# A two-pass MLP on one core: the second eighth's weights split piece by piece, the first pass's DMA queue written out by hand, and four buffers for the gated weights

## The chip, the core and the metric

The kernel runs on one core of a Trainium2 chip. The core has TensorE (matrix products into eight PSUM banks), VectorE, ScalarE and GpSimd (element-wise work; in the profile DVE, ACT and POOL) and SyncE, whose queue (SPq in the profile) issues nearly every DMA. The metric is the device time in microseconds, the median of several runs.

## The reference

One transformer-like layer with 1024 tokens and width 1024, all in float32. The change lies in its last third, the MLP (c and the six modulation rows come from a small projection at the start):

```python
h = (_rms(x) * (1.0 + scale_f) + shift_f)
u = jnp.square(jax.nn.relu(jnp.einsum('bsd,df->bsf', h, w_mlp_in[l])))   # 1024x1024 by 1024x4096
x = x + gate_f * jnp.einsum('bsf,fd->bsd', u, w_mlp_out[l])              # 1024x4096 by 4096x1024
```

## The kernel before, in words

**A float32 product** is made of three passes of TensorE: each operand is split into a rounded part and a rest (`split_w`, L137: a ScalarE cast, L138, then a VectorE subtraction, L139), and hi by hi, hi by lo and lo by hi are summed in PSUM.

**The first pass** computes `u` in eight eighths of 512 columns. An eighth is one step of Strassen's scheme in Winograd's form on 2x2 blocks: seven products (`one`, `two`, `six`, `five`, `seven`, `three`, `four`, L1124 to L1185) of 24 matmuls of 128x128 by 128x512 each instead of eight products, with sums of blocks before (`tees`, L1142; L1156, L1157) and after. The four blocks of an eighth's weights are called 11, 12, 21 and 22, `b["2"]` is a further sum. The activations' seven operands (A11, A12, S1 to S4, A22) are made once and kept, split, in 14 of 18 large buffers (tag `s8`, 8 KB in each partition). The weights' split pairs have two buffers (`mr`), the loaded blocks 21, 12 and 22 five (`f4`), block 11 two (`raw`). The results `ua` and `ub` (`s8`) go to DRAM (`put`, L1120).

**The start** of the first pass overlaps the end of the projection before it: its last two groups, `woB0` and `woB1`, are evicted from PSUM (L955), added to x by GpSimd (L956), and the rows of x are normalised (`h2_norm`, L974) and turned by TensorE (`h2_turn`, L992) three tokens' blocks at a time (`HI`, tokens' blocks 5, 6 and 7) between the first products of eighths 0 and 1. In that stretch, L1239 to L1251, the orders of TensorE, ScalarE and VectorE are written out by hand; instructions from outside of it may be put between.

**Beside the first pass** GpSimd multiplies the rows of `w_mlp_out` by the gate row (`gate_load`, `gate_times`, `gate_store`, L1190 to L1209), in 32 pieces of 128 rows: a 512 KB load, two or three multiplications or subtractions of 128x512, two 256 KB stores to `wd_d`. It has two buffers, and two pieces in every three products.

**The order of everything else** is chosen by a list scheduler on a simulated timeline: whatever the program's order offers first and the simulation holds ready is next on its engine. That holds for SyncE's queue too, but for the loads and stores of the gates, whose order among themselves is the program's. An engine then works its instructions in that order and waits at each for its operands. A load waits in the queue for its buffer to be free.

**The second pass** does the same on `u` and `wd_d`, four quarters of seven products of 48 matmuls (`product`, L1286; matmuls at L1304). Loads of its operands (`load`, L1271) and of x (`x2b`) begin as the buffers of the first pass come free; `t_two` (L1330) is a difference that GpSimd makes for the third product.

## Time and profile before

| | |
|---|---|
| median of 3 runs | 1380.03 us (1377.92 to 1384.39) |
| profiled execution | 1383.38 us, of which 1381.6 us are the span from first to last instruction |
| busy in the span | TensorE 93%, VectorE 71%, ScalarE 37%, GpSimd 33% |
| mean granted TensorE clock | 0.975 of 2.4 GHz |

The profile gives one execution. Times within it are microseconds from the span's start. A row of a timeline gives start, duration, engine, line, operation, written tile <- read tiles, shape, count, and in brackets how long the engine had been idle and what released it. A matmul's own duration (0.39) is longer than its distance to the next one, since matmuls are pipelined.

### The profile page before, as it was taken

How to read it: one execution, taken by the hardware profiler on the slowest of the kernel's cores; microseconds unless marked ns; L12 is line 12 of the kernel's file. 1: busy time of each engine (PE TensorE's matmuls, PEld its weight loads, DVE VectorE, ACT ScalarE, POOL GpSimd, SP SyncE). 2: the span in 40 equal slices, each digit the busy share in tenths (PEclk: the TensorE clock that was granted, in tenths of full speed). 3: DMA queues.
4: the chain of work that ended last, by engine and by line, in shares of the span. 5: the costliest groups of instructions: out<-in, count | busy, mean ns of one | idle time of the engine just before them, and what ended most of it. 6: DMA issues, size and time to landing. Idle time of an engine off the chain costs nothing. (4 is left out here: it accounts for less than half of the span.)

```text
span 1381.6 us, 16679 instructions
## 1 busy us (share of the span) xinstructions
PE 1288.2 (93%) x6131; PEld 1042.5 (75%) x6131; DVE 974.7 (71%) x1486; ACT 515.8 (37%) x801; POOL 460.4 (33%) x364
## 2 busy tenths in 40 slices
PE   5899899999999899999976898889999899999998
PEld 3678777888888666678864786678888778888887
DVE  6758897476754367753687574668867989888883
ACT  3642212343333366652544432222334242424240
POOL 1129451156622013322340034644553714050500
PEclk9899999999999999999997999999999999999999
DMA  9656566534357574832550348667669450514202
GB/s 292 187 126 164 151 171 141 132 100 139 115 168 174 140 166 116 291 138 78 181 168 16 107 160 263 218 221 234 234 208 354 179 215 29 199 46 152 92 31 92
DMA packets 123601, 220.51 MB, mean 160 GB/s; under 512 B 9896, under 2 KB 70376, under 8 KB 117888
## 3 DMA queue, kind: packets, MB, share of 16 engines
q1 hardware_dynamic: 100640, 202.68, 47.8%
q10 hardware_dynamic: 22880, 16.78, 3.9%
q8 instruction: 48, 0.79, 0.2%
q14 instruction: 33, 0.27, 0.1%
HBM read 159.55 MB, written 48.34 MB: 150 GB/s over the span
## 5 line engine op out<-in xcount | busy, mean ns | idle before, releaser
L1304 PE MATMUL V<-sb,sa 128*128 128x512 f32 x768 | 180.3, 392 | 6.0 <-DVE sb L139 4.7
L1201 POOL TENSOR_TENSOR wg<-wg,gf 128x512 f32<-128x512 f32 x64 | 107.5, 1703 | 223.1 <-DMA wg<-in_w_mlp_out_dram 120.0
L1304 PEld LDWEIGHTS V<-sb,sa 128*128 128x128 f32 x768 | 145.1, 189 | 37.8 <-DVE sb L139 5.9
L135 POOL TENSOR_TENSOR sm<-sm 128x8 f32<-128x8 f32 (+2 forms) x48 | 62.0, 1298 | 138.5 <-DVE sm L253 48.8
L1304 PE MATMUL U<-sb,sa 128*128 128x512 f32 x384 | 88.8, 389 | 0.0
L1304 PEld LDWEIGHTS U<-sb,sa 128*128 128x128 f32 x384 | 72.1, 188 | 14.9
L138 ACT CAST sb<-b 128x1024 fp32r<-128x1024 f32 x40 | 40.7, 1052 | 103.5 <-PE V L1304 57.5
L238 DVE SCALAR_TENSOR_TENSOR wa<-wa,sm 128x128 f32<-128x128 f32 (+1 forms) x154 | 72.4, 470 | 3.3
L1330 POOL TENSOR_TENSOR wdt<-b,t 128x1024 f32<-128x1024 f32 x8 | 24.3, 3060 | 136.9 <-DMA b<-wd_d 136.9
L1282 DVE TENSOR_TENSOR x2b<-V,x2b 128x512 f32<-128x512 f32 x64 | 42.5, 683 | 35.0 <-PE V L1304 35.0
L711 DVE CUSTOM_DVE_ANT_0 p<-S,wh 128x512 f32<-128x512 f32 (+3 forms) x96 | 49.9, 552 | 24.1 <-DMA wh<-nc_d 16.2
L139 DVE TENSOR_TENSOR sa<-a,sa 128x2048 fp32r<-128x2048 f32 x20 | 60.3, 3015 | 4.2 <-ACT sa L138 4.1
L139 DVE TENSOR_TENSOR sb<-b,sb 128x1024 fp32r<-128x1024 f32 x40 | 55.4, 1410 | 3.5 <-ACT sb L138 1.6
L701 POOL TENSOR_SCALAR_AFFINE_SELECT wh<-wh 128x128 f32<-128x128 f32 x64 | 18.2, 293 | 108.2 <-DVE sm L711 53.1
L723 ACT ACTIVATE p<-p,sm 128x1024 f32<-128x1024 f32 (+7 forms) x64 | 49.1, 770 | 4.4 <-DVE sm L719 3.7
L707 PE MATMUL S<-kt,qt 128*128 128x512 f32 (+3 forms) x96 | 38.7, 408 | 9.2 <-DVE sm L711 6.6
L138 ACT CAST sa<-a 128x2048 fp32r<-128x2048 f32 x20 | 38.2, 1911 | 22.3 <-DVE a L1327 11.0
L1304 PE MATMUL W<-sb,sa 128*128 128x512 f32 x192 | 45.1, 389 | 0.0
L743 PE MATMUL pt<-ident,p 128*128 128x128 f32 x288 | 40.6, 282 | 2.6 <-ACT p L723 2.6
L743 PEld LDWEIGHTS pt<-ident,p 128*128 128x128 f32 x288 | 31.7, 142 | 13.4 <-issue 8.1
L1304 PEld LDWEIGHTS W<-sb,sa 128*128 128x128 f32 x192 | 36.1, 188 | 7.5
L752 PE MATMUL av<-pT,fv 128*64 128x256 f32 (+1 forms) x320 | 40.2, 373 | 0.0
(391 smaller groups left out, 3449.3 us busy)
## 6 DMA issues: line engine op xcount, KB each, us to landing
wu<-in_w_mlp_in_dram SPq DMA_DIRECT2D x32, 512.0 KB, 4.5
wg<-in_w_mlp_out_dram SPq DMA_DIRECT2D x32, 512.0 KB, 4.8
wd_d<-wg SPq DMA_DIRECT2D x64, 256.0 KB, 3.6
a<-u_d SPq DMA_DIRECT2D x12, 1024.0 KB, 6.4
b<-wd_d SPq DMA_DIRECT2D x12, 1024.0 KB, 7.1
wa<-in_w_ada_dram ACTq DMA_DIRECT2D x10, 1024.0 KB, 5.7
wam<-in_w_ada_dram SPq DMA_DIRECT2D x16, 512.0 KB, 7.7
u_d<-ua SPq DMA_DIRECT2D x16, 512.0 KB, 3.0
```

Source lines behind the costliest of these rows:

```text
L135: G.tensor_tensor(ap, ap, mhalf.to_broadcast([P, n]), op=ALU.pow)
L138: A.copy(h_ap, raw_ap)
L139: eng.tensor_tensor(l_ap, raw_ap, f32(h_ap), op=ALU.subtract)
L238: V.scalar_tensor_tensor(w[:, 0], w[:, j], c_act[:, j : j + 1], w[:, 0], op0=ALU.mult, op1=ALU.add)
L707: T.matmul(sp[n], qt[:, n, dg], kt[:, n, c_], start=True, stop=False)
L711: V.tensor_tensor_reduce(ps[n][:, c_], sp[n], wh[:, n, c_], -1.0, 3.4e38, op0=ALU.add, op1=ALU.min, accum_out=mcs[n][c0 // CH])
L723: A.activation(ps[n][:, :W], ps[n][:, :W], AF.Exp, bias=mcs[n][0], scale=-1.0, accum_out=den[:, 2 * i + n : 2 * i + n + 1],)
L743: T.transpose(tp[:, n, i * P : (i + 1) * P], ps[i][n][:, j * P : (j + 1) * P], ident)
L752: T.matmul(av[own, at], fox_pair_of("fv", pr)[:, j, n * FD : (n + 1) * FD], pts[j][:, n, i0 * P :], start=(j == 0), stop=(j == 2 * gg + 1),)
L1201: G.tensor_tensor(w[:, hf], w[:, hf], gf[hf], op=ALU.mult)
L1282: V.tensor_tensor(xs, banks[i], xs, op=ALU.add)
L1304: T.matmul(banks[i], sa[pa][:, a, ii], sb[pb_][a // 2][:, a % 2, :], start=(first and a == 0 and m == 0), stop=(a == 3 and m == 2), skip_g ...
```

## The change

It edits five things. (1) `xn`, the normalised rows of tokens' blocks 0 to 4, takes buffers of tag `r2` (four) and no longer of `t2` (three), which the evictions of `woB` use too; the gate row `gf` goes the other way. (2) Eighth 1's block 22 and its sum `2` are kept as two half-size tiles each in `r2`, no longer in one `s8` buffer, so their load, splits and sums run in halves (`minus`). (3) In the stretch written by hand, eighth 1's splits of 11 and 21 stand right behind the work that frees their buffers, eighth 0's split of `2` at the end, and the sums that end `two` (`end_two`) behind the stretch. (4) From the fifth product on, the order of SyncE's queue is written out too: in each step the gate's store of two steps before, the gate's load, the weights' loads, and then the result stores of the step before. The gates take one piece in every step, from step 12 to step 45, in four buffers (two in one `s8` buffer, two in `r2`), and each load is two of 256 KB. (5) In the second pass `t1` and `b22` are loaded before `a12` and `b21`, `t_two` is made before the first product, and two of the four loads of x move behind the load of `a22`.

```diff
--- before.py
+++ after.py
@@ -978,7 +978,7 @@
         A.activation(ra([P, D], f"x2sq{t}"), xt, AF.Square, accum_out=rr)
         V.tensor_scalar(rr, rr, 1.0 / D, EPS, op0=ALU.mult, op1=ALU.add)
         rsqrt_(rr, 1)
-        xn = [t2([P, CH], f"xn{t}{n}") for n in range(2)] if t < 5 else None
+        xn = [r2([P, CH], f"xn{t}{n}") for n in range(2)] if t < 5 else None
         if xn is None:
             v = s8([P, D], f"xn{t}")
             V.tensor_scalar(v, xt, rr, None, op0=ALU.mult)
@@ -1070,6 +1070,19 @@
     NE = 8
     W2 = 2 * P
 
+
+    stores = []
+
+    def pieces(w):
+        return w if isinstance(w, list) else [w]
+
+    def minus(dst, u, v):
+
+        if any(isinstance(w, list) for w in (dst, u, v)):
+            dst, u, v = (w if isinstance(w, list) else [w[:, 0:2], w[:, 2:4]] for w in (dst, u, v))
+        for a, b, c_ in zip(pieces(dst), pieces(u), pieces(v)):
+            V.tensor_tensor(a, b, c_, op=ALU.subtract)
+
     class Eighth:
         def __init__(self, e):
             self.e = e
@@ -1081,17 +1094,25 @@
                 if name in names:
                     r, c_ = int(name[0]) - 1, int(name[1]) - 1
                     if self.e == 1 and name == "22":
-                        both = s8([P, 2, 4, W2], "wu1_22")
-                        self.b["2"], w = both[:, 0], both[:, 1]
+                        w = self.halves(name)
                     else:
                         w = make([P, 4, W2], f"wu{self.e}_{name}")
                     self.b[name] = w
                     at = self.e * CH + c_ * W2
-                    Q.dma_start(w, wup_v[:, 4 * r : 4 * r + 4, at : at + W2])
+                    n = 4 // len(pieces(w))
+                    for i, v in enumerate(pieces(w)):
+                        Q.dma_start(v, wup_v[:, 4 * r + n * i : 4 * r + n * i + n, at : at + W2])
+
+        def halves(self, name):
+
+            return [r2([P, 2, W2], f"wu{self.e}_{name}{i}") for i in range(2)]
 
         def halve(self, name):
             s = self.split[name] = mr([P, 2, 4, W2], f"wu{self.e}s{name}", F32R)
-            split_w(self.b[name], s[:, 0], s[:, 1])
+            w = pieces(self.b[name])
+            n = 4 // len(w)
+            for i, v in enumerate(w):
+                split_w(v, s[:, 0, n * i : n * i + n], s[:, 1, n * i : n * i + n])
 
         def product(self, left, name, banks, first):
             if name not in self.split:
@@ -1119,7 +1140,7 @@
 
         def put(self, n, st):
             at = self.e % 2 * 2 * CH
-            Q.dma_start(u_d[self.e // 2][n][:, at : at + 2 * CH], st.rearrange("p f c -> p (f c)"))
+            stores.append(lambda: Q.dma_start(u_d[self.e // 2][n][:, at : at + 2 * CH], st.rearrange("p f c -> p (f c)")))
 
         def one(self):
             self.X = [self.make[f](f"X{self.e}_{f}") for f in range(2)]
@@ -1132,19 +1153,22 @@
         def two(self):
             Y = [self.make[2 + f](f"Y{self.e}_{f}") for f in range(2)]
             self.product("A12", "21", Y, True)
+            self.Y = Y
             if self.e > 1:
                 self.tees()
+                self.end_two()
+
+        def end_two(self):
             for f in range(2):
-                V.tensor_tensor(self.c11[:, f], Y[f], self.c11[:, f], op=ALU.add)
+                V.tensor_tensor(self.c11[:, f], self.Y[f], self.c11[:, f], op=ALU.add)
                 self.square(self.c11, f)
             self.put(0, self.c11)
 
         def tees(self):
             b = self.b
             V.tensor_tensor(b["12"], b["12"], b["11"], op=ALU.subtract)
-            if self.e != 1:
-                b["2"] = ra([P, 4, W2], f"wt{self.e}")
-            V.tensor_tensor(b["2"], b["22"], b["12"], op=ALU.subtract)
+            b["2"] = self.halves("2") if self.e == 1 else ra([P, 4, W2], f"wt{self.e}")
+            minus(b["2"], b["22"], b["12"])
 
         def six(self):
             self.product("S2", "2", self.X, False)
@@ -1153,8 +1177,8 @@
             for f in range(2):
                 A.copy(self.c12[:, f], self.X[f])
             b = self.b
-            V.tensor_tensor(b["11"], b["2"], b["11"], op=ALU.subtract)
-            V.tensor_tensor(b["21"], b["21"], b["2"], op=ALU.subtract)
+            minus(b["11"], b["2"], b["11"])
+            minus(b["21"], b["21"], b["2"])
 
         def five(self):
             self.Z = [self.make[2 + f](f"Z{self.e}_{f}") for f in range(2)]
@@ -1190,23 +1214,26 @@
     def gate_load(n):
         if not gf:
             for hf in range(2):
-                gf.append(r2([P, CH], f"gf{hf}"))
+                gf.append(t2([P, CH], f"gf{hf}"))
                 Q.dma_start(gf[hf], rows_d[1, hf * CH : (hf + 1) * CH].partition_broadcast(P))
-            wg.append(s8([P, 2, 2, CH], "wg"))
-        tc.keep_in_program_order(Q.dma_start(wg[0][:, n % 2].rearrange("p h c -> p (h c)"), wdn_v[:, n, :]))
+            t = s8([P, 2, 2, CH], "wg")
+            wg.extend([t[:, i, hf] for hf in range(2)] for i in range(2))
+            wg.extend([r2([P, CH], f"wg{i}{hf}") for hf in range(2)] for i in range(2))
+        for hf in range(2):
+            Q.dma_start(wg[n % 4][hf], wdn_v[:, n, hf * CH : (hf + 1) * CH])
 
     def gate_times(n):
-        w = wg[0][:, n % 2]
+        w = wg[n % 4]
         for hf in range(2):
-            G.tensor_tensor(w[:, hf], w[:, hf], gf[hf], op=ALU.mult)
+            G.tensor_tensor(w[hf], w[hf], gf[hf], op=ALU.mult)
         if n % 4 < 2:
-            G.tensor_tensor(w[:, 1], w[:, 1], w[:, 0], op=ALU.subtract)
+            G.tensor_tensor(w[1], w[1], w[0], op=ALU.subtract)
 
     def gate_store(n):
         e, c_, f = n // 4, n // 2 % 2, n % 2
         at = (e % 2 * 2 + f) * CH
         for hf in range(2):
-            tc.keep_in_program_order(Q.dma_start(wd_d[e // 2][2 * c_ + hf][:, at : at + CH], wg[0][:, n % 2, hf]))
+            Q.dma_start(wd_d[e // 2][2 * c_ + hf][:, at : at + CH], wg[n % 4][hf])
 
     eighths = [Eighth(e) for e in range(NE)]
     e0, e1 = eighths[:2]
@@ -1218,7 +1245,7 @@
         steps += [lambda e=e, n=n: getattr(eighths[e], n)() for n in ("one", "two", "six", "five", "seven", "three", "four")]
     side = [[] for _ in range(len(steps) + 4)]
     for n in range(32):
-        at = 2 + n // 2 * 3 + n % 2
+        at = 12 + n
         for d, what in ((0, gate_load), (1, gate_times), (2, gate_store)):
             side[at + d].append(lambda what=what, n=n: what(n))
 
@@ -1237,32 +1264,39 @@
     for e in (e0, e1):
         e.load(("12", "22"))
     with tc.manual_schedule(engines={ENG.PE, ENG.Activation, ENG.DVE}):
-        for n, t in enumerate(HI):
-            if n == 0:
-                e0.one()
-            elif n == 1:
-                e0.two()
-            else:
-                e1.one()
-            h2_turn(t, xn[t])
-            make_s2(t)
-            if n == 0:
-                e0.tees()
+        e0.one()
+        h2_turn(HI[0], xn[HI[0]])
+        make_s2(HI[0])
+        e0.tees()
+        e1.halve("11")
+        e0.two()
+        h2_turn(HI[1], xn[HI[1]])
+        make_s2(HI[1])
+        e1.halve("21")
+        e1.one()
+        h2_turn(HI[2], xn[HI[2]])
+        make_s2(HI[2])
         e1.two()
+        e0.halve("2")
     e1.tees()
+    e0.end_two()
     split_part("S1", "r21", whole)
+    e1.end_two()
     split_part("A22", "r22", whole)
     r22, r12, r11 = (h2r[r] for r in ("r22", "r12", "r11"))
     V.tensor_tensor(r22, r22, r11, op=ALU.subtract)
     split_part("S3", "r22", whole)
     V.tensor_tensor(r12, r12, r11, op=ALU.subtract)
     split_part("S4", "r12", whole)
-    for n, step in enumerate(steps):
-        step()
-        for what in side[n]:
+    with tc.manual_schedule(engines={ENG.SP}):
+        for n, step in enumerate(steps):
+            due = list(stores)
+            stores.clear()
+            step()
+            for what in side[n] + due:
+                what()
+        for what in sum(side[len(steps) :], []) + stores:
             what()
-    for what in sum(side[len(steps) :], []):
-        what()
 
     x2b = []
     for q in range(4):
@@ -1313,21 +1347,24 @@
         def two(name):
             return lambda g: blk[name][:, 2 * g : 2 * g + 2]
 
-        for name in ("a11", "b11", "a12", "b21"):
+        for name in ("a11", "b11", "t1", "b22", "a12", "b21"):
             load(name)
+
+        def load_x2(n):
+            x2b.append(s8([P, 2, D], f"x2b{n}"))
+            Q.dma_start(x2b[n].rearrange("p i d -> p (i d)"), x2_d[n])
+
+        t_two = [raw([P, 2, CH], f"wdt{q}{g}") for g in range(2)]
+        for g in range(2):
+            G.tensor_tensor(t_two[g], two("b22")(g), two("t1")(g), op=ALU.subtract)
         X = [lower[i](f"V{q}_{i}") for i in range(4)]
         product(1, blk["a11"], two("b11"), X, True, 0)
         if q == 0:
-            for n in range(4):
-                x2b.append(s8([P, 2, D], f"x2b{n}"))
-                Q.dma_start(x2b[n].rearrange("p i d -> p (i d)"), x2_d[n])
-        for name in ("s1", "t1", "b22"):
-            load(name)
+            load_x2(0)
+            load_x2(1)
+        load("s1")
         add(X, 0, 0)
         V.tensor_tensor(blk["a11"], blk["s1"], blk["a11"], op=ALU.subtract)
-        t_two = [raw([P, 2, CH], f"wdt{q}{g}") for g in range(2)]
-        for g in range(2):
-            G.tensor_tensor(t_two[g], two("b22")(g), two("t1")(g), op=ALU.subtract)
         Y = [upper[i](f"W{q}_{i}") for i in range(4)]
         product(2, blk["a12"], two("b21"), Y, True, 1)
         add(Y, 0, 0, True)
@@ -1335,6 +1372,9 @@
             G.tensor_tensor(two("b11")(g), t_two[g], two("b11")(g), op=ALU.subtract)
             G.tensor_tensor(two("b21")(g), two("b21")(g), t_two[g], op=ALU.subtract)
         load("a22")
+        if q == 0:
+            load_x2(2)
+            load_x2(3)
         product(6, blk["a11"], lambda g: t_two[g], X, False, 0)
         add(X, 0, 1)
         V.tensor_tensor(blk["a12"], blk["a12"], blk["a11"], op=ALU.subtract)

```

## Rows read from the trace of the kernel before

**Rows 1.** Page, part 1: busy us, share of the span, instructions of each engine.

```profile
PE 1288.2 (93%) x6131; PEld 1042.5 (75%) x6131; DVE 974.7 (71%) x1486; ACT 515.8 (37%) x801; POOL 460.4 (33%) x364
```

**Rows 2.** Chain that ended last, in time: start us, us, what; its last product.

```profile
1366.99 10.89 PE V L1304 x48
```

**Rows 3.** Busy time per stage of the MLP: us, engines (instructions), clock, DMA share, GB/s.

```profile
703.99:761.26 57.27, 37.46 (x145) 28.43 (x145) 47.09 (x60) 26.64 (x42) 9.21 (x7) 0.82 0.20 68
761.26:814.88 53.62, 50.13 (x218) 40.23 (x217) 28.18 (x31) 21.90 (x32) 0.00 (x0) 1.00 0.37 120
814.88:950.03 135.15, 120.54 (x506) 98.02 (x504) 91.17 (x81) 34.89 (x45) 75.83 (x46) 0.95 0.71 235
950.03:1064.27 114.24, 114.24 (x506) 94.63 (x504) 87.51 (x83) 39.47 (x50) 51.89 (x30) 1.00 0.71 246
1064.27:1117.55 53.28, 47.32 (x199) 37.78 (x197) 48.68 (x33) 21.64 (x16) 28.34 (x10) 0.97 0.53 209
1117.55:1381.60 264.05, 260.32 (x1147) 215.28 (x1147) 209.86 (x176) 82.09 (x64) 60.76 (x18) 1.00 0.28 103
```

**Rows 4.** Timeline, TensorE: start, us, line, what, count, [idle before <-releaser].

```profile
705.40 5.72 PE L1103 MATMUL X<-h2A,wu0s 128*128 128x512 f32 x24 [1.41 <-DVE gawoB L955]
713.78 1.06 PE L999 MATMUL h2p<-ident,xn 128*128 128x128 f32 x8 [2.66 <-ACT x2sq L978]
714.60 5.74 PE L1103 MATMUL Y<-h2A,wu0s 128*128 128x512 f32 x24
...
730.97 8.63 PE L1103 MATMUL X<-h2A,wu1s 128*128 128x512 f32 x24 [9.76 <-ACT wu1s L138]
...
746.13 1.22 PE L1103 MATMUL Y<-h2A,wu1s 128*128 128x512 f32 x2 [5.66 <-ACT wu1s L138]
...
843.72 7.43 PE L1103 MATMUL X<-h2S,wu2s 128*128 128x512 f32 x20 [6.02 <-DVE wu2s L139]
...
915.66 7.33 PE L1103 MATMUL Y<-h2A,wu4s 128*128 128x512 f32 x20 [3.81 <-DVE wu4s L139]
...
1091.49 6.44 PE L1304 MATMUL V<-sb,sa 128*128 128x512 f32 x20 [3.69 <-DVE sb L139]
```

**Rows 5.** Timeline, VectorE, first pass.

```profile
697.04 0.68 DVE L955 TENSOR_TENSOR gawoB<-po_woB,gm 128x512 f32<-128x512 f32 x1
...
723.17 1.28 DVE L1138 TENSOR_TENSOR ua<-Y,ua 128x512 f32<-128x512 f32 x2
...
730.95 1.22 DVE L139 TENSOR_TENSOR wu1s<-wu,wu1s 128x1024 fp32r<-128x1024 f32 x1 [0.26 <-ACT wu1s L138]
...
841.31 1.22 DVE L1147 TENSOR_TENSOR wt<-wu,wu 128x1024 f32<-128x1024 f32 x1 [11.05 <-DMA wu<-in_w_mlp_in_dram]
...
881.86 1.37 DVE L139 TENSOR_TENSOR wu3s<-wu,wu3s 128x1024 fp32r<-128x1024 f32 x1 [3.36 <-ACT wu3s L138]
890.64 2.34 DVE L1147 TENSOR_TENSOR wt<-wu,wu 128x1024 f32<-128x1024 f32 x1 [7.41 <-DMA wu<-in_w_mlp_in_dram]
```

**Rows 6.** Timeline, ScalarE, first pass.

```profile
793.87 1.07 ACT L1154 COPY ub<-X 128x512 f32<-128x512 f32 x2 [2.10 <-DVE wu1s L139]
```

**Rows 7.** Timeline, SyncE's DMA queue, first pass.

```profile
835.46 0.45 SPq L1090 DMA_DIRECT2D wu<-in_w_mlp_in_dram  x1
...
883.96 0.64 SPq L1090 DMA_DIRECT2D wu<-in_w_mlp_in_dram  x1
```

**Rows 8.** Timeline, GpSimd, start of the second pass.

```profile
1079.98 7.08 POOL L1330 TENSOR_TENSOR wdt<-b,t 128x1024 f32<-128x1024 f32 x2 [5.59 <-DMA b<-wd_d]
```

**Rows 9.** Instructions of tile wg and of line 1147: duration ns min/median/max.

```profile
L1201 POOL TENSOR_TENSOR wg<-wg,gf x64: 1262/1730/2697, 817.5 to 1073.1; 128x512 f32<-128x512 f32 x64
...
L1147 DVE TENSOR_TENSOR wt<-wu,wu x7: 1224/1226/2337, 722.0 to 1009.5; 128x1024 f32<-128x1024 f32 x7
```

**Rows 10.** DMA issues: line, count, KB each, median us to landing.

```profile
wg<-in_w_mlp_out_dram SPq DMA_DIRECT2D x32, 512.0 KB, 4.8
wd_d<-wg SPq DMA_DIRECT2D x64, 256.0 KB, 3.6
```

## What the change should do

> **What bounds the kernel now.** I read the page first. TensorE is the busiest engine by far, with VectorE behind it [rows 1], so the question is where TensorE idles or runs slowly. The chain that ended last answers for the second pass: it is one product after another, 10.89 us for 48 matmuls, so 0.227 us each [rows 2]. A product of the first pass (24 matmuls) therefore needs 5.44 us. With that price I cut the MLP at the ends of products and set each stage against its need [rows 3]:
>
> - A, 703.99 to 761.26: five products (27.2 us) and 24 transposes. Eight transposes take 0.82 us (713.78 to 714.60) [rows 4], so 2.5 in all. The stage needs 29.7 us and takes 57.3. **Lost: 27.6.**
> - B, to 814.88: nine products, 49.0 of 53.6. **Lost: 4.7.**
> - C, to 950.03: 21 products, 114.2 of 135.2. **Lost: 20.9.**
> - To 1064.27: 21 products in 114.24. Nothing lost.
> - D, to 1117.55: 197 matmuls of the second pass, 44.7 of 53.3. **Lost: 8.6.**
> - The rest is 1147 matmuls, 260 us, in 260.3 of TensorE time. Nothing lost.
>
> So 61.8 us can be had at most. The timeline of TensorE shows what each loss hangs on, and a second price with it: after idling 9.76 us the next 24 matmuls took 8.63 us instead of 5.72, and after 3.81 us the next 20 took 7.33 [rows 4]. In A and C the granted clock is 0.82 and 0.95 of 2.4 GHz [rows 3], so part of the time passed at the lower level, 1.2 GHz. An idle stretch there costs up to twice its length.
>
> **Stage A, the start.** The three large waits are 1.41 + 2.66 us at its head, 9.76 for eighth 1's split of 11 and 5.66 for its split of 21 [rows 4]; they are 19.5 of the 27.6, and the lower clock is nearly all of the other 8.1. VectorE is packed in the same stretch, 47.1 us of 57.3 [rows 3], so what counts is what stands ahead of each split. The split of 11 starts on VectorE at 730.95. The eleven instructions from 723.17 up to it (seven lines of the timeline: eighth 0's end of `two`, the turn of token block 6 and its sums, two sums of eighth 0) are 7.8 us [rows 5], and the new order puts the written ones among them behind the split. Edit 1 moves more away: the eviction of `woB0` runs at 697.04 [rows 5], although the group behind it (72 matmuls, 16.3 us) ended at 703.99, so its own matmuls were done before 688: the rows `xn` hold the buffers. With `xn` in `r2`, up to three evictions of 0.68 us go out earlier, 2.0 us. That puts the split at about 721 (730.95 - 7.8 - 2.0), while TensorE, without the 1.41 and with half of the 2.66, arrives at about 718 (703.99 + 2 x 5.44 + 2 x 0.82 + 1.3). A wait of 2 to 3 us remains where 9.76 was. Then eighth 1's `one` (5.4), the turn (0.8), `two` (5.4) and eighth 0's `six` (5.4) follow nearly without a wait, since the split of 21 now stands ahead of `one`'s evictions: the stage's work ends at about 740 (721 + 17.1, and some 2 us for splits that follow a turn). I take 6.5 lost of 27.6, **gain 21.1**. Bounds: 27.6 if VectorE keeps up; about 11 if free instructions (eighth 1's `tees`, the two sums) fill in ahead of the splits, since 5 us of them bring back a wait beyond the 3.81 us after which the clock fell.
>
> **Stage B.** Eighth 1's copies `ub` ran at 793.87, only after a split of eighth 1 that freed a large buffer [rows 6], and its `seven` was put behind `three`. Edit 2 frees that buffer from the start. Its price is halves: 2 x 0.68 instead of 1.22 us, 0.14 for each of one split and three sums, on a VectorE that is busy 28 of 54 us in B [rows 3], so nothing on the path; were that cover gone, 0.6 us. **Gain 2.7** of 4.7 (bounds 0 and 4.7).
>
> **Stage C, the fixed queue.** Two kinds of wait stand here. Eighth 3's sum at 841.31 held VectorE for 11.05 us waiting for block 22 [rows 5], whose load was issued at 835.46 [rows 7], behind gate stores; a split that TensorE needed was queued behind the sum, and TensorE idled 6.02 us and then took 7.43 for 20 matmuls [rows 4]. In the new order that load comes at the step after its buffer is freed, with the gates ahead of it two steps old, and it is needed four steps (22 us) later. The second kind is another one: eighth 4's block 22 was issued at 883.96, 0.7 us after the split that freed its buffer (881.86 + 1.37), yet the sum at 890.64 waited 7.41 us [rows 5, 7]. There the queue was prompt, and VectorE's order put the sum too early. The new queue helps that only as far as the simulated and the true landing come together. So I take back two thirds: 7.5 lost of 20.9, **gain 13.4** (bounds 0 and 20.9).
>
> Cost: the gates now take a piece per product, not two in three. A piece is 2.5 instructions of 1.73 us on GpSimd [rows 9], 4.3 us of the 5.44. It moves 1 MB; with 0.29 MB each of weights and results per product that is 1.6 MB in 5.44 us, about 295 GB/s (246 in the stretch without loss [rows 3]). SyncE issues twice as many gate loads, of 256 KB instead of 512. At 0.45 us for an issue [rows 7] a step with five issues takes 2.3 us of its 5.44, which is hidden; without the cover it would be 0.45 per load. The nearest row for a 256 KB transfer is the gate's store, 3.6 us to landing, against 4.8 for 512 KB [rows 10], so nothing is added for that. A result store now stands one step later and holds its large buffer 5.4 us longer; with 14 of 18 kept for activations and one for gates, three are left for results where two are in use at a time from eighth 2 on, so nothing. It waits in the queue for the sums that follow its product; behind it stand the next step's gate store and loads, which have two steps in hand.
>
> VectorE pays: its block sums take between 1.22 and 2.34 us [rows 9], the long ones beside GpSimd. With half as many gates again, I charge **2.5 us** for steps 12 to 45, between 0 (VectorE has 26.7 us idle in the 114.24 of the clean stretch [rows 3]) and 13.5 (third rival). "SBUF — State Buffer" of the Trainium skill, section "Who interferes with whom", has a rule that speaks against this edit: a GpSimd instruction and a VectorE instruction with two SBUF inputs exclude each other, and the later one is blocked until the other has ended. By that rule the charge is 13.5 and the time 1350; by the clean stretch it is near nothing and the time 1337.
>
> **Stage D.** The wait of 3.69 us at 1091.49 is for a split of `t_two` [rows 4], which GpSimd made only at 1079.98 because it waited for `b22` [rows 8], loaded last. Loaded fourth, and with two megabytes of x out of its way, `t_two` is done before the first product starts. `a12` and `b21` now come after it, but they have a product's 10.9 us more. Ending the gates six steps before the pass ends takes them out of this crowd. **Gain 6.1** of 8.6 (bounds 2 and 8.6).
>
> **Sum.** 21.1 + 2.7 + 13.4 - 2.5 + 6.1 = 40.8 us. The profiled execution took 1383.4 (span 1381.6 and 1.8 around it), 3.4 above the median of 1380.0. From the median: **1339 us**.
>
> **Rivals.** *Second: VectorE's order keeps C.* The 7.41 us wait with a prompt load speaks for it, the clean 114.24 us under the same scheduler against. C loses 20.9 as before: 1339 + 13.4 = 1352.
>
> *Third: the gates are too dense.* If GpSimd and a VectorE instruction that reads two SBUF tensors exclude each other, one step needs 2.5 x 1.26 on GpSimd and, on VectorE, 11 block sums and splits of 1.22 and eight instructions of 0.68 in seven steps, 2.7: 5.9 us in 5.44, 13.5 us over 32 steps. 2.34 against 1.22 and 2.70 against 1.26 [rows 9] look like that; that nothing was lost to 1064.27 is against it only at the old density (4.8 of 5.44). With 13.5 lost instead of 2.5 the time is 1350.
>
> *Fourth: the start stays bound by VectorE*, gain 11 instead of 21: 1349.
>
> *The other side: SyncE in lockstep.* Each gate store now stands in the queue two steps (10.9 us) behind its load, and everything later waits behind it. Load 4.8 plus GpSimd 4.3 is 9.1, so it fits. If landings grow to 12 us, a pair of steps takes 16.3, 5.4 too much, 87 over 32 steps, less the 22 us by which the weights are ahead: 65 lost, 1404. It turns the sign from landings of 10.5 us on ((40.8 + 22) / 16 = 3.9 per pair). Medians of 3.6 and 4.8 at up to 246 GB/s [rows 3, 10] are far from that; 295 GB/s is not seen in a stretch that long.
>
> *The edits do little:* the gaps go on elsewhere and the time stays within 0.5%, which is about what a measurement of this kernel can tell from no change: 1380. *All gaps close:* 1323.
>
> **How the numbers follow.** Forecast (1328 to 1347) 0.48, second 0.14, third 0.12, fourth 0.05, all gaps closed 0.10, no change 0.03, lockstep 0.08. The range from 1322 to 1364 leaves out the last two and about half of the "all closed" case, so it holds some 0.84; the forecast's own range is 1328 to 1347. All but the last two are faster by more than 0.5%: faster 0.89, same 0.03, slower 0.08.
>
> **What would show it.** Eighth 1's `one` starts on TensorE near 720 and the granted clock stays at 1.00 from there on. Eighth 0's `six` ends near 740. No sum of lines 1144 or 1147 waits over 3 us for a weight load; GpSimd's gate work ends some 35 us before the second pass starts. The split of `t_two` isn't what the third product waits for. It is wrong if VectorE's waits for weights persist or if SyncE's queue waits for GpSimd for longer than a product.

## The result, and the profile after

The changed kernel takes 1365.2 us (median of three runs, 1364.2 to 1367.3) against 1380.0: a ratio of 0.9889, with a 95% interval of 0.9862 to 0.9917. So it gained 14.8 us where 40.8 were forecast, and the time lies 1.2 us outside the range. Its profiled execution has a span of 1363.5 us, 18.1 below that of before; the gains of the stages are worked out between these two spans.

The same windows as in [rows 3], cut at the same places of the program, but that A now ends with the sixth product (`Z<-h2S,wu0s` starts) and eighths 2 to 7 are two windows of three eighths each:

```profile
703.86:757.66 53.80, 42.01 (x169) 33.12 (x168) 45.16 (x61) 31.13 (x49) 8.00 (x6) 0.87 0.24 83
757.66:801.18 43.52, 43.52 (x193) 36.04 (x192) 27.94 (x32) 19.74 (x29) 0.00 (x0) 1.00 0.34 112
801.18:929.11 127.93, 119.23 (x505) 97.43 (x504) 90.55 (x82) 34.99 (x45) 77.16 (x48) 0.95 0.75 254
929.11:1052.00 122.89, 116.57 (x506) 95.51 (x504) 84.10 (x78) 42.39 (x51) 57.94 (x35) 0.99 0.76 270
1052.00:1077.73 25.73, 23.77 (x102) 18.54 (x100) 25.66 (x19) 8.11 (x7) 12.65 (x4) 1.00 0.45 183
1077.73:1363.50 285.77, 282.04 (x1243) 233.22 (x1243) 223.35 (x193) 92.15 (x71) 58.04 (x18) 1.00 0.27 103
```

With the prediction's price (5.44 us for a product, 2.5 for the 24 transposes) they read so; each "lost" comes from one execution. A needs 35.1 us and loses 18.7; in the kernel before the sixth product ran without a loss, so its 27.6 stand beside that. B needs all of its 43.5. Eighths 2 to 4 lose 13.7 of 127.93, and eighths 5 to 7 lose 8.65, where before they lost nothing. The second pass takes 311.5 us instead of 317.3 (both last windows, and in [rows 3] the last two).

| stage | lost before | lost after | gain | forecast |
|---|---|---|---|---|
| A, start | 27.6 | 18.7 | 8.9 | 21.1 |
| B | 4.7 | 0.0 | 4.7 | 2.7 |
| C, eighths 2 to 4 | 20.9 | 13.7 | 7.2 | 13.4 |
| eighths 5 to 7 (denser gates) | 0.0 | 8.65 | -8.65 | -2.5 |
| D, second pass | 8.6 | 2.8 | 5.8 | 6.1 |

They add up to 18.0 of the 18.1 us between the spans. Eighths 2 to 7, over which the fixed queue and the denser gates work together, lose 22.3 us, against 20.9 before.

**Where A still waits.** TensorE's timeline, which answers to [rows 4]:

```profile
714.10 1.97 PE L999 MATMUL h2p<-ident,xn 128*128 128x128 f32 x8 [3.57 <-DVE xn L984]
715.72 7.53 PE L1124 MATMUL Y<-h2A,wu0s 128*128 128x512 f32 x24
...
728.16 5.29 PE L1124 MATMUL X<-h2A,wu1s 128*128 128x512 f32 x22 [3.15 <-DVE wu1s L139]
733.29 1.03 PE L999 MATMUL h2p<-ident,xn 128*128 128x128 f32 x8
738.21 8.14 PE L1124 MATMUL Y<-h2A,wu1s 128*128 128x512 f32 x24 [3.89 <-ACT h2r L1004]
```

Eighth 1's `one` starts in earnest at 728.16, not near 720, and the granted clock does not stay at 1.00 behind it (0.95 in eighths 2 to 4). And VectorE's timeline of that stretch (L1169 and L1084 are the sums of weight blocks, `tees` and those behind `six`; L1163 is `end_two`; L1026 and L1027 the sums of the turned rows):

```profile
705.64 1.22 DVE L139 TENSOR_TENSOR wu0s<-wu,wu0s 128x1024 fp32r<-128x1024 f32 x1 [1.70 <-ACT wu0s L138]
706.78 0.68 DVE L955 TENSOR_TENSOR gawoB<-po_woB,gm 128x512 f32<-128x512 f32 x1
...
718.06 1.28 DVE L1084 TENSOR_TENSOR wu<-wu,wu 128x512 f32<-128x512 f32 x2
720.61 0.69 DVE L1163 TENSOR_TENSOR ua<-Y,ua 128x512 f32<-128x512 f32 x1 [1.27 <-PE Y L1124]
721.22 0.68 DVE L1026 TENSOR_TENSOR h2r<-h2r,h2r 128x512 f32<-128x512 f32 x1
...
726.89 1.22 DVE L139 TENSOR_TENSOR wu1s<-wu,wu1s 128x1024 fp32r<-128x1024 f32 x1
728.02 1.36 DVE L1006 TENSOR_SCALAR h2r<-h2p,sm 128x128 f32<-128x128 f32 x4
729.30 1.21 DVE L1084 TENSOR_TENSOR wu<-wt,wu 128x1024 f32<-128x1024 f32 x1
730.43 1.22 DVE L1084 TENSOR_TENSOR wu<-wu,wt 128x1024 f32<-128x1024 f32 x1
731.57 1.28 DVE L1084 TENSOR_TENSOR wu<-wu,wu 128x512 f32<-128x512 f32 x2
732.77 0.68 DVE L1026 TENSOR_TENSOR h2r<-h2r,h2r 128x512 f32<-128x512 f32 x1
```

The written order holds among its own instructions, but others stand between them. Ahead of the split of 11 (726.89) stand eighth 1's sums (718.06) and eighth 0's `end_two`, for which VectorE waits 1.27 us while the ready L1026 stands behind it. Behind the split, four more sums (3.7 us) stand between the turn of the second row and its L1026; the split of 21, and ScalarE's evictions of the third turn (the 3.89 us wait), come later by them. At the head, eighth 0's split of 21 waits for its late load and holds the last three evictions of `woB1`, and with them the rows that TensorE turns after its 3.57 us wait.

**Where eighths 3 to 6 wait.** There is one gap in each of them, at the product `three`. In eighth 3, on TensorE, VectorE and SyncE's queue:

```profile
871.18 7.33 PE L1124 MATMUL Z<-h2S,wu3s 128*128 128x512 f32 x20 [3.46 <-DVE wu3s L139]
```

```profile
866.57 2.35 DVE L1084 TENSOR_TENSOR wt<-wu,wu 128x1024 f32<-128x1024 f32 x1 [6.81 <-DMA wu<-in_w_mlp_in_dram]
868.85 2.28 DVE L139 TENSOR_TENSOR wu3s<-wu,wu3s 128x1024 fp32r<-128x1024 f32 x1
```

```profile
854.07 0.33 SPq L1143 DMA_DIRECT2D u_d<-ua  x1
854.50 1.22 SPq L1236 DMA_DIRECT2D wd_d<-wg  x2
855.76 1.30 SPq L1223 DMA_DIRECT2D wg<-in_w_mlp_out_dram  x2
857.46 1.57 SPq L1236 DMA_DIRECT2D wd_d<-wg  x2
859.08 0.96 SPq L1223 DMA_DIRECT2D wg<-in_w_mlp_out_dram  x2
860.13 0.38 SPq L1104 DMA_DIRECT2D wu<-in_w_mlp_in_dram  x1
```

The sum is eighth 4's and needs eighth 4's block 22; the split behind it is eighth 3's, for `three`. The load was issued at 860.13, 3.85 us after the split that freed its buffer ended (853.97 + 2.31 = 856.28), behind the gate stores and gate loads of two steps. Landing and the start of the sum took 6.4 more, the sum 2.35, the split 2.28. That is a chain of 14.9 us, of which 11.4 were covered by products: the gap is 3.5, and the 20 matmuls behind it take 7.33 us, as those behind the gaps in [rows 4] did. In eighth 4 the same chain is 17.3 us and the gap 5.24.

The two steps' gate transfers were late themselves, because a result store stands in the queue ahead of them. SyncE had issued nothing for 3.8 us before 854.07, and from there to the load it took 6.1 us (8.3 to 9.7 in eighths 4 to 6). Over eighths 2 to 7 (800 to 1052 us) SyncE's queue waited longer for VectorE's results than for the gates (total us, times, longest):

```profile
SPq L1143 <- DVE ua L1139: 74.7, 12, 10.4
SPq L1236 <- POOL wg L1230: 21.6, 11, 3.1
```

No run moved the result stores, so what this wait costs is not shown.

Landings grew: the page's DMA issues, which answer to [rows 10]; the weight loads took 4.5 before.

```profile
wg<-in_w_mlp_out_dram SPq DMA_DIRECT2D x64, 256.0 KB, 5.2
wu<-in_w_mlp_in_dram SPq DMA_DIRECT2D x31, 512.0 KB, 6.3
```

**D** gained what was forecast. `t_two` is made at 1040.99, eleven us before the second pass begins, and no wait of the third product for a split is longer than 0.40 us where one was 3.69 [rows 4, 8]:

```profile
1040.99 5.21 POOL L1359 TENSOR_TENSOR wdt<-b,t 128x1024 f32<-128x1024 f32 x2 [34.51 <-DMA b<-wd_d]
```

### The profile page after: what moved, and what is told of

The parts are those of the page before. It is cut to its first block, busy times and chain, and to the rows that moved or that the text cites. A ratio compares the mean times of both kernels' runs of the same rounds, so it can differ in the third digit from the quotient of the medians.

```text
span 1363.5 us, 16691 instructions
## 1 busy us (share of the span) xinstructions
PE 1284.4 (94%) x6131; PEld 1041.8 (76%) x6131; DVE 962.5 (71%) x1491; ACT 516.3 (38%) x803; POOL 448.9 (33%) x364
## 4 chain that ended last, share of the span: by engine, by line
PE 40%; DVE 6%; DMA 4%; POOL 3%; issue 2%; SPq 1%; ACT 1%; DVEq 0%; POOLq 0%; ACTq 0%
PE V L1338 12%; PE U L1338 6%; PE X L1124 5%; PE Z L1124 4%; DMA wg<-in_w_mlp_out_dram 3%; PE W L1338 2%; POOL wg L1228 2%; PE Y L1124 2%; DMA wu<-in_w_mlp_in_dram 2%; PE po_woA L950 1%; PE po_woA L949 1%; PE po_woA L951 1%; PE po_woB L950 1%; PE po_woB L951 1%; PE po_woB L949 1%
## 5 line engine op out<-in xcount | busy, mean ns | idle before, releaser
L1338 PEld LDWEIGHTS U<-sb,sa 128*128 128x128 f32 x384 | 72.1, 188 | 14.9
L1359 POOL TENSOR_TENSOR wdt<-b,t 128x1024 f32<-128x1024 f32 x8 | 19.5, 2453 | 146.4 <-DMA b<-wd_d 109.9
L139 DVE TENSOR_TENSOR sa<-a,sa 128x2048 fp32r<-128x2048 f32 x20 | 53.5, 2674 | 8.1 <-PE V L1338 5.6
L701 POOL TENSOR_SCALAR_AFFINE_SELECT wh<-wh 128x128 f32<-128x128 f32 x64 | 18.1, 293 | 107.4 <-DVE sm L711 53.0
L1373 POOL TENSOR_TENSOR b<-b,wdt 128x1024 f32<-128x1024 f32 x8 | 27.1, 3392 | 48.8 <-DVE sb L139 48.8
L743 PEld LDWEIGHTS pt<-ident,p 128*128 128x128 f32 x288 | 31.7, 142 | 13.4 <-issue 8.1
```

The source lines that it names most:

```text
L139: eng.tensor_tensor(l_ap, raw_ap, f32(h_ap), op=ALU.subtract)
L743: T.transpose(tp[:, n, i * P : (i + 1) * P], ps[i][n][:, j * P : (j + 1) * P], ident)
L1338: T.matmul(banks[i], sa[pa][:, a, ii], sb[pb_][a // 2][:, a % 2, :], start=(first and a == 0 and m == 0), stop=(a == 3 and m == 2), skip_g ...
```

## The experiments

Twelve kernels, each against the kernel before on its own chip. A ratio of 0.9889 is the changed kernel; unless said otherwise, each is that kernel with one edit. "Lost" is worked out from windows cut as above, in the one profiled execution of each kernel. The kernels before had medians of 1379.9 to 1382.6 on their chips, so two medians of different chips are compared to some 3 us.

### Eighths 2 to 7: VectorE's order, the queue, or the gates

**`p1_pin_sums`**, VectorE's order alone:

```diff
+    PIN = range(2, 8)
...
         def tees(self):
-            V.tensor_tensor(b["12"], b["12"], b["11"], op=ALU.subtract)
+            first = V.tensor_tensor(b["12"], b["12"], b["11"], op=ALU.subtract)
+            if self.e in PIN:
+                tc.keep_in_program_order(first)
...
-            minus(b["2"], b["22"], b["12"])
+            minus(b["2"], b["22"], b["12"], self.e in PIN)
```

> The changed kernel, with the two sums of `tees` of eighths 2 to 7 held on VectorE behind the split of their own eighth's block 21; the queue is untouched. First theory (VectorE's order: the second sum stands ahead of the previous eighth's split of 22 and waits 7 to 10 us there for a load that isn't needed yet): the four waits of 2.4 to 5.2 us at `three` go, and of the 22 us that eighths 3 to 6 lose about 4 remain, so about 1347 us. Second theory (the load stands too late in the queue): the load is as late as before, but nobody waits for it, so it says 1347 too and is told apart by the run with the earlier load. Third theory (gates too dense, GpSimd slows VectorE): the gaps turn up at other splits, 1358 or more.

Measured: 1348.4 us, ratio 0.9728 (0.9671 to 0.9785). Two sums held at their place are worth 17 us, more than the whole change. Its windows of eighths 2 to 4 and 5 to 7:

```profile
803.48:919.50 116.02, 115.08 (x506) 94.38 (x505) 94.36 (x81) 35.22 (x45) 79.65 (x47) 1.00 0.84 277
919.50:1036.71 117.21, 115.45 (x505) 94.21 (x504) 96.02 (x82) 42.62 (x51) 64.94 (x36) 1.00 0.79 285
```

1.8 and 3.0 us are lost instead of 13.7 and 8.65; the second pass takes 311.4 us, as in the changed kernel. The load is issued as late as ever (863.14 in the same eighth) and the sums still take 2.2 us beside GpSimd, but they stand behind the splits and nothing waits:

```profile
866.09 2.30 DVE L139 TENSOR_TENSOR wu3s<-wu,wu3s 128x1024 fp32r<-128x1024 f32 x1 [4.30 <-ACT wu3s L138]
...
885.19 2.19 DVE L1084 TENSOR_TENSOR wt<-wu,wu 128x1024 f32<-128x1024 f32 x1
```

**`c1_load22_first`**, the place of that load in the queue:

```diff
-        at = 7 if e == 2 else 10 + 7 * (e - 3) + 4
-        side[at].append(lambda e=e: eighths[e].load(("22",)))
+        at = 7 if e == 2 else 10 + 7 * (e - 3) + 3
+        side[at].insert(0, lambda e=e: eighths[e].load(("22",)))
```

> The changed kernel with the load of block 22 one step earlier in the queue and ahead of that step's gate transfers; VectorE's order is left to the scheduler, which answers by putting the sum ahead of the split of `seven` as well. Second theory: the load comes 4 to 7 us earlier, three quarters of the 22 us come back, about 1349 us. First theory: the sum moves forward as the load does and waits some 6 us in its new place, where two splits stand behind it; no gain or a loss, 1360 to 1375. Third theory: no change, 1363 to 1367.

Measured: 1347.6 us, 0.9757 (0.9713 to 0.9800); eighths 2 to 7 lose 8.7 us (118.02 and 119.12 for the two windows). The profiled execution is the longest of four, 1355.5 us, 7.8 above the median, so this loss may be above the usual one. The load is issued 2.2 us behind the result store in each of eighths 3 to 6, 4.3 to 6.0 us earlier in its eighth than in the changed kernel. The sum still stands ahead of the split and still waits for the load, 4.56 us in eighth 3, yet TensorE waits 0.71 where it waited 3.46:

```profile
862.91 1.23 DVE L1084 TENSOR_TENSOR wt<-wu,wu 128x1024 f32<-128x1024 f32 x1 [4.56 <-DMA wu<-in_w_mlp_in_dram]
864.05 2.48 DVE L139 TENSOR_TENSOR wu3s<-wu,wu3s 128x1024 fp32r<-128x1024 f32 x2
```

So VectorE's order is not a cause by itself: it makes the load's lateness TensorE's, and either repair takes most of the loss away.

**`c2_no_gate_work`** leaves GpSimd's multiplications of the rows of `w_mlp_out` out (the second pass then runs on unscaled weights); their loads and stores stay.

```diff
     def gate_times(n):
-        w = wg[n % 4]
-        for hf in range(2):
-            G.tensor_tensor(w[hf], w[hf], gf[hf], op=ALU.mult)
-        if n % 4 < 2:
-            G.tensor_tensor(w[1], w[1], w[0], op=ALU.subtract)
+        pass
```

> The changed kernel without GpSimd's multiplications and subtractions of the gates: loads and stores stay as they are, so the second pass runs on weights that are not scaled. Third theory: block sums on VectorE are back at 1.22 us, the gaps at `three` close, about 1343 us. First and second theory: the queue no longer waits for GpSimd (30 us in 23 waits), so block 22 is issued some 3 us earlier and the waits of 7 to 10 us become 3 to 6; half of the 22 us comes back, about 1354 us.

Measured: 1347.0 us, 0.9733 (0.9694 to 0.9771); eighths 2 to 7 lose 3.5 us (115.11 and 116.85). The sum of eighth 3 still waits 6.50 us for its load, but all block sums are short, and the loads of block 22 leave 1.2 to 3.4 us sooner in their eighths, since SyncE need not wait for GpSimd at a store. The run takes both away at once and does not tell their shares apart. Tile `wt`, min/median/max, first without the gate work, then with it:

```profile
L1084 DVE TENSOR_TENSOR wt<-wu,wu x7: 1216/1225/1226, 726.7 to 982.4; 128x1024 f32<-128x1024 f32 x7
```

```profile
L1084 DVE TENSOR_TENSOR wt<-wu,wu x7: 1218/1655/2352, 725.7 to 1000.8; 128x1024 f32<-128x1024 f32 x7
```

The rule weighed in the prediction ("SBUF — State Buffer" of the Trainium skill, "Who interferes with whom") has its mark here: up to 1.1 us more for a sum beside GpSimd, and none when GpSimd is idle. But in `p1_pin_sums` the sums and the gates meet no less (median 2.2 us) and 4.8 us are lost in all, so here the long sums cost time mainly where the late load has used up the slack.

**`c4_store_later`**, SyncE's wait for GpSimd at the gate stores:

```diff
-        for d, what in ((0, gate_load), (1, gate_times), (2, gate_store)):
+        for d, what in ((0, gate_load), (1, gate_times), (3, gate_store)):
```

> Each gate block is stored three steps behind its load instead of two, so that SyncE, standing at the store, need not wait for GpSimd's multiplications; nothing else changes. First theory (the load of block 22 is late by the sum of queue, landing and slowed VectorE, and the queue's part is SyncE standing at stores that wait for GpSimd): that load is issued 3 to 5 us sooner in each eighth, eighths 2 to 7 lose about 8 us instead of 22, time 1349. Second theory (the queue is held by the number of transfers ahead of the load, or by the wait moving to the gate loads, which need the landed store of the buffer's last use): eighths 2 to 7 lose 18 to 22, time 1362.

Measured: 1359.3 us, 0.9851 (0.9817 to 0.9885); eighths 2 to 7 lose 15.6 us. Neither number came. In eighth 3 the load is no sooner: it is issued at 861.69, 6.3 us behind the result store (6.1 before) and 4.08 after the split that frees its buffer (857.61; 3.85 before). What shortened that gap to 2.74 is the sum, which here took 1.23 us instead of 2.35. In eighths 4 to 6 the first theory's step came, in part: the load follows the result store by 5.5 to 5.7 us instead of 8.3 to 9.7.

```profile
861.69 0.42 SPq L1104 DMA_DIRECT2D wu<-in_w_mlp_in_dram  x1
```

```profile
868.33 1.23 DVE L1084 TENSOR_TENSOR wt<-wu,wu 128x1024 f32<-128x1024 f32 x1 [7.24 <-DMA wu<-in_w_mlp_in_dram]
```

```profile
871.81 4.84 PE L1124 MATMUL Z<-h2S,wu3s 128*128 128x512 f32 x20 [2.74 <-DVE wu3s L139]
```

The 20 matmuls behind this gap of 2.74 us took 4.84 us, and not 7.33 as behind one of 3.46. The length of the gap alone does not decide that: in eighth 4 of the same run 20 took 6.45 behind a gap of 1.94. The later stores took back 6.7 us of the 22.3, about a third.

**`g1_old_density`**, gates two in three steps as before, but each five steps later than in the kernel before, so that the last ones run into the second pass:

```diff
-        at = 12 + n
+        at = 7 + n // 2 * 3 + n % 2
```

> The 32 gate blocks at the density of the kernel before, two in three steps (from step 7 to 55) instead of one in every step, under the fixed queue. First theory (denser gate work is one of the three parts of the delay, on the queue and on VectorE's instructions): eighths 2 to 7 lose 10 to 14 us instead of 22, time 1353 to 1357 if the last stores don't hold up the second pass. Second theory (a block in two steps of three still meets the load of block 22 in most eighths): the loss stays at 18 to 22, time 1362.

Measured: 1363.1 us, 0.9876 (0.9837 to 0.9915): no gain that can be told from the changed kernel's. The windows show why:

```profile
799.61:926.66 127.05, 117.97 (x506) 95.22 (x504) 87.11 (x83) 34.90 (x45) 67.24 (x40) 0.99 0.73 244
926.66:1041.62 114.96, 114.56 (x505) 94.44 (x504) 85.28 (x76) 39.26 (x48) 63.01 (x38) 1.00 0.74 259
1041.62:1361.30 319.68, 307.92 (x1345) 253.38 (x1343) 254.75 (x212) 103.65 (x82) 84.33 (x27) 0.99 0.33 126
```

Eighths 5 to 7 lose 0.7 us again, as before the change, and eighths 2 to 4 still lose 12.8: so the denser gates' bill is 8.8 us. The second pass takes it back: 319.68 us instead of 311.5, with a wait of 3.40 in its first product, while the last gates and their stores crowd its loads. The last gate store is issued at 1072.2, 31 us into the second pass (before the change 11 us into it, in the changed kernel 40 us ahead of it). So D's gain needs the gates' early end, though `t_two` is made before the second pass here too; what `t_two`'s own loads earn no run shows.

**`u_sp_free_queue`**, the fixed order of loads and stores taken away. It is not the queue of the kernel before, where the gates' loads and stores kept their order among themselves:

```diff
-    with tc.manual_schedule(engines={ENG.SP}):
+    with ExitStack():
         for n, step in enumerate(steps):
```

> The changed kernel with the order of SyncE's loads and stores in the first pass left to the scheduler. First theory (in eighths 2 to 7 the fixed order gained nothing in sum: 22.3 us lost with it, 20.9 without): 1360 to 1372 us, and the loads of block 22 are issued at other times but the loss in those eighths stays at 18 to 26 us. Second theory (the fixed order earned part of the gain, and the denser gates took it back): 1378 or more, the loss in those eighths over 33 us.

Measured: 1378.7 us, 0.9977 (0.9957 to 0.9997). The time is the second theory's, the losses in eighths 2 to 7 (25.8) are the first's. The queue's 13 us lie elsewhere, in B, in the window 760.08 to 811.03:

```profile
760.08:811.03 50.95, 46.68 (x194) 37.76 (x192) 31.22 (x29) 19.23 (x29) 21.66 (x15) 0.93 0.79 266
```

Left to itself the queue draws the gates forward (GpSimd is busy 21.66 us in B, where it has nothing to do in the changed kernel) and puts eighth 2's block 22 behind them; VectorE's sum waits for it and a split that TensorE needs stands behind the sum, the same pattern:

```profile
791.29 1.22 DVE L1084 TENSOR_TENSOR wt<-wu,wu 128x1024 f32<-128x1024 f32 x1 [3.36 <-DMA wu<-in_w_mlp_in_dram]
...
796.06 2.28 DVE L139 TENSOR_TENSOR wu0s<-wu,wu0s 128x1024 fp32r<-128x1024 f32 x1
```

```profile
798.39 7.36 PE L1124 MATMUL X<-h2A,wu0s 128*128 128x512 f32 x20 [3.83 <-DVE wu0s L139]
```

B loses 7.4 us by that, A 0.9, eighths 2 to 7 lose 3.5 more than with the fixed order; the MLP's first product began 1.5 us later in this execution. These are the 13.3 us between the spans.

### The start

**`u_start_old_order`**, the written order of the kernel before under the new buffers:

```diff
-        e1.halve("11")
-        e0.two()
-        h2_turn(HI[1], xn[HI[1]])
-        make_s2(HI[1])
-        e1.halve("21")
-        e1.one()
...
+            if n == 0:
+                e0.one()
+            elif n == 1:
+                e0.two()
+                e0.end_two()
+            else:
+                e1.one()
+            h2_turn(t, xn[t])
+            make_s2(t)
...
         e1.two()
-        e0.halve("2")
+        e1.end_two()
     e1.tees()
-    e0.end_two()
...
-    e1.end_two()
```

> The changed kernel with the start's hand-written order of the kernel before: the splits of eighth 1's blocks and of eighth 0's sum stand where the products call them, and the sums behind the second product right behind it. First theory (the order written out at the start earned the 8.9 us that the first six products gained): 1374 us, with a loss near 27 us up to the end of the six products. Second theory (the gain there comes from the buffers and the earlier loads, and the order adds nothing, because sums stand ahead of the splits in either): 1365, a loss of 18 to 20.

Measured: 1374.4 us, 0.9944 (0.9922 to 0.9967). A loses 27.9 us (63.04 for the six products), what it lost before, with the old waits for eighth 1's two splits, 7.97 and 5.65 us [rows 4]:

```profile
730.50 8.12 PE L1124 MATMUL X<-h2A,wu1s 128*128 128x512 f32 x24 [7.97 <-ACT wu1s L138]
...
745.15 1.22 PE L1124 MATMUL Y<-h2A,wu1s 128*128 128x512 f32 x2 [5.65 <-ACT wu1s L138]
```

The order written by hand earned all that A gained, 9.2 us between these two traces; with the rows `xn` in other buffers alone A loses what it lost before. Seven kernels with the new order and no edit to the start lose 16.2 to 19.6 us in A (the changed one 18.7, `g1_old_density` 16.2, `c1_load22_first` 19.6), so the gain stands clear of that spread, and a difference of 3 us between two of them does not.

**`a1_hold_start`** holds the free sums of the start (eighth 1's `tees`, both `end_two`, the sums behind both `six`) at their place with the same call as above.

> The changed kernel with eighth 1's `tees`, the sums that end `two` of eighths 0 and 1 and the two sums of `six` of both held in program order on VectorE, so that they no longer stand among the hand-ordered turns and splits of the start. If these sums delay the start: eighth 1's split of 11 ends near 723.7 instead of 728.1 and that of 21 some 8 us earlier, the stage that loses 18.7 us loses about 10, about 1356 us. If the start is bound by the late weight load of eighth 0's block 21 or by the banks that eighth 1's `two` shares with the turn: 1362 to 1367.

Measured: 1363.3 us, 0.9855 (0.9819 to 0.9891), no gain in time. The first two windows:

```profile
707.27:749.81 42.54, 34.28 (x149) 26.41 (x147) 36.55 (x50) 26.20 (x46) 7.09 (x6) 0.96 0.22 72
749.81:799.43 49.62, 48.81 (x213) 39.74 (x214) 36.45 (x42) 23.51 (x32) 0.00 (x0) 1.00 0.36 119
```

The first `five` now begins inside eighth 1's `six`, so the cut between A and B falls some 20 matmuls earlier, and only the sum of the two counts: they lose 13.5 us instead of 18.7. Only 1.8 of these 5.2 us reach the end of B, since the first product began 3.4 us later in this execution (707.27; it also did in kernels that touch nothing of the start, 707.84 with the sums of eighths 2 to 7 held). The first four products did get faster: eighth 1's `two` starts 26.0 us after the first product and takes 5.78 us, where it started 34.4 after it and took 8.14. The wait for the split of 11 is 0.32 us instead of 3.15. But `six`, `five` and what follows then wait for their splits, at most 1.50 us at a time.

```profile
733.25 5.78 PE L1128 MATMUL Y<-h2A,wu1s 128*128 128x512 f32 x24 [1.21 <-ACT h2r L1004]
```

The span is 1.9 us shorter, and eighths 2 to 7, untouched here, lose 22.2.

**`h1_move_split21`**, the split that waits at the head:

```diff
     e0.halve("11")
-    e0.halve("21")
...
         e0.one()
+        e0.halve("21")
```

> Only the split of eighth 0's block 21 moves, from ahead of the hand-written stretch to behind eighth 0's first product. First theory (the start's first stall is VectorE waiting for that block's load in front of the evictions of the first transposes): the 3.57 us gap ahead of the transposes of the first row falls to about 1 us, and the time to 1362. Second theory (the start is bound further down, by the chain of splits and sums on VectorE): the gap moves to the next turn or the next product, the first three stages lose 18 to 19 us as before, time 1365.

Measured: 1360.0 us, 0.9837 (0.9808 to 0.9867), nearer the first theory's time; the interval just meets that of the changed kernel. The head's 3.57 us wait fell to 1.22, and that of 3.15 for the split of 11 is gone; in their place stand 3.29 for the moved split and, at the third turn's evictions, 4.50 instead of 3.89. A loses 15.3 us (50.43 for the six products) instead of 18.7, but only 0.9 less than the least of the seven kernels above, and the untouched eighths 2 to 7 lose 20.0 here: a stage differs by 2 to 3 us from one kernel to the next without an edit to it. That the waits moved is shown; that A gained by it is not.

### Together

**`ph_sums_head`** (sums of eighths 2 to 7 and the head), **`pa2_pin_all`** (these and the start's sums) and **`b1_sums_on_gpsimd`** (these, and the subtractions behind the start's two `six` on GpSimd):

```diff
-            i = V.tensor_tensor(a, b, c_, op=ALU.subtract)
+            i = (G if pool else V).tensor_tensor(a, b, c_, op=ALU.subtract)
...
-            minus(b["11"], b["2"], b["11"], self.e < 2)
-            minus(b["21"], b["21"], b["2"], self.e < 2)
+            minus(b["11"], b["2"], b["11"], self.e < 2, self.e < 2)
+            minus(b["21"], b["21"], b["2"], self.e < 2, self.e < 2)
```

> The pinned sums of eighths 2 to 7 together with the moved split of eighth 0's block 21; the sums of the start are left to the scheduler. First theory (both gains are separate): eighths 2 to 7 lose about 5 us, the start 15, time 1345. Second theory (the sooner start only meets the later gaps, as with the split moved alone, where the two stages of eighths 2 to 7 shifted by 2 to 4 us either way): 1348, as with the sums alone.

> Three edits together: the sums of all eighths from the second on kept at their place in the program, the sums of the start held there too, and the split of eighth 0's block 21 moved behind the first product. First theory (the gaps of eighths 2 to 7 and those of the start are separate and add up): eighths 2 to 7 lose about 5 us as with their sums alone held, the start 10 to 13, time 1340. Second theory (the start's time only moves from gap to gap, as its own edit of 2 us showed): 1347, with a start that loses 17 again.

> The three edits together, and the six subtractions that follow the third product of eighths 0 and 1 moved from VectorE to GpSimd, which is idle from 731 to 761 us of the run with the three edits, while VectorE is busy 29.9 of those 30 us. First theory (what is left of the start's loss, 12.4 us, is VectorE's work): 5.0 us of work leave it, the start loses 8 to 9, time 1338 to 1340. Second theory (GpSimd's subtractions slow VectorE's while they run, as the gates' do in the later eighths, 1.22 to 2.2 us each, and take 2.4 us each themselves): the start loses 12 or more, time 1343 to 1346.

Measured: 1346.1 (0.9750, 0.9710 to 0.9789), 1343.2 (0.9714, 0.9680 to 0.9747) and 1341.7 us (0.9717, 0.9686 to 0.9748). Eighths 2 to 7 lose 4.2, 6.0 and 5.4 us, A and B 15.5, 12.4 and 13.5. In the windows the gains stand side by side. In the time they are not shown to add up: all three ratios lie within the interval of the held sums alone (0.9671 to 0.9785). In the last one GpSimd takes 3.8 us for each of the four small subtractions:

```profile
744.45 15.16 POOL L1084 TENSOR_TENSOR wu<-wu,wu 128x512 f32<-128x512 f32 x4 [17.82 <-issue]
```

From the first matmul of `six` to eighth 2 TensorE needed 57.8 us where it needed 60.6 in `pa2_pin_all`, but ahead of it 3.5 us were lost (a wait of 3.18 instead of 1.21 at the third turn, then 24 matmuls in 7.33 instead of 5.78). The 1.5 us between the two medians cannot be told from nothing. All three kernels beat both the kernel before and the changed one, as the held sums alone did.

## Why the prediction was wrong

**What held.** The cut into stages and the price of a product stood: every stage's time is its need plus its gaps and the slower matmuls behind some of them. (For waits of 3.69 to 9.76 us [rows 4] put the cost, slow matmuls included, at 1.3 to 1.7 times the wait, where the prediction says up to twice.) D came in the forecast size (5.8 for 6.1); `g1_old_density` shows that the gates' early end was needed for it, and no run shows the part of `t_two`'s loads. The sign was right. SyncE in lockstep did not come: its longest wait for a gate was 3.1 us. Two figures of the rivals are off by their own terms, and nothing turns on it: the exclusion comes to about 13 us and not 13.5, and all gaps closed to 1318 or, with the charge of 2.5, 1321 and not 1323.

**Step 1, A at 21.1 us: failed, 8.9 measured.** The mechanism is the stated one (the order of the splits; `u_start_old_order`), but the step "the new order puts the written ones among them behind the split" took the written order for VectorE's whole order. The free sums filled in ahead of the splits, as the lower bound of 11 and the fourth rival said, and the gain fell even below that bound, with the head's late load as a further wait. Two of its smaller terms were nothing: the 2.0 us from `xn`, and the quick rest of the stage, where the third turn's evictions now came late. That the free sums hold up eighth 1's products is shown (`a1_hold_start`: `two` starts 8.4 us sooner behind the first product). That they are the whole shortfall is not: holding them cut A's and B's loss by 5.2 us, not by 12, and the time by nothing that can be told. TensorE then waited for the splits of `six` and `five`, with VectorE busy for 29.8 of 30 us (733 to 763); that its amount of work is the reason is argued. The fourth rival had been given 0.05.

**Step 2, B at 2.7: 4.7 came**, but not from the buffer alone: with the buffers and a free queue B loses 7.4. The fixed order keeps the gates out of B.

**Step 3, C at 13.4 and the denser gates at 2.5: together 10.9 expected, -1.4 measured.** The prediction saw the pattern (a sum placed too early on VectorE, a split behind it), gave it 0.14 as the second rival, and took back two thirds by the queue. What the runs show is a chain: load late in the queue, landing, sum, split. Three premises failed. The load was to be needed four steps (22 us) later; but its sum stood on VectorE ahead of a split of the eighth before, so the cover was 11.4 us. The gates ahead of the load were to be two steps old; but SyncE had stood at the result store ahead of them, whose place was priced at nothing, and the load came 6.1 to 9.7 us behind that store. And the charge of 2.5 us looked at the busy time of VectorE and GpSimd and found cover, not at the load's chain: SyncE's waits at gate stores are 6.7 us of the loss (`c4_store_later`), and the density as a whole is 8.8, most of it the same gap in eighths 5 to 7 (`g1_old_density`). Cutting the chain at any one of three places (order, load's place, gate work) gives 14 to 19 us back. Without the fixed queue the kernel is 13.5 us slower (`u_sp_free_queue`), close to the 13.4 forecast, but that is chance: only 3.5 of it lie in eighths 2 to 7, and 7.4 in B, where the fixed order keeps the gates out.

**The sum.** Taken away singly, the start's order costs 9.2 us and the fixed queue 13.5. If they add, they are 22.7 of a gain of 14.8, so the rest of the change cost some 8 us, with the denser gates' 8.8 us in eighths 2 to 7 in it; the prediction had the rest gain 6.3 (2.7 + 6.1 - 2.5). By the ratios, each on its own chip, they are 7.6 and 12.1 of 15.3, and the rest cost some 4.

**Open** is why A and B still lose 12 to 20 us in every version with the new order and the fixed queue. A VectorE that is full there speaks for its amount of work, but moving 5 us of it away gave 2.8 at most. Open, too, is what the result stores' wait for VectorE costs.

## What to carry to other kernels

An order written out for one engine or one stretch is a promise about those instructions alone: look in the static order for free instructions between them, above all ones that wait for a late load, since an in-order engine makes everything behind them wait. A chain of queue, landing, sum and split with 11 to 12 us of cover (eighths 3 and 4) costs nothing up to that and every microsecond beyond, so price it as a chain and not by the engines' busy shares. And a late load can be repaired at either end: two sums kept at their place, or the load one step earlier, each gave more than the whole change had (1348.4 and 1347.6 us).

## What the runs showed of the hardware

Landing times followed the traffic and the order in the queue as well as the size (medians). Gate loads of 512 KB took 4.8 us before; halved to 256 KB they took 4.2 at the old density (`g1_old_density`) and 5.2 at the new one. The unchanged 512 KB weight loads took 4.5 before, 5.2 with the denser gates in a free queue (`u_sp_free_queue`), and 6.1 and 6.3 in the fixed queue at the old and the new density. The core moved 254 to 270 GB/s in eighths 2 to 7 instead of 235 to 246 [rows 3]. A GpSimd subtraction of 128x512 took 1.55 us on average among the gates of the changed kernel and 3.8 at the start of `b1_sums_on_gpsimd`, where VectorE was busy for 28.0 of 30 us (729 to 759). And a queue left to the scheduler was 13.5 us slower through work that it did too early, not too late: the gates in B.
